# Experts' transposes inside the preceding products, and five weight splits behind the first fetch

## The chip, the cores and the metric

The kernel runs on one core of a Trainium2 chip. A core has TensorE (PE; its weight loads are shown as PEld), VectorE (DVE), ScalarE (ACT), GpSimd (POOL) and SyncE (SP, which here only issues DMAs). Each engine works through its own queue in order. The metric is the time of one execution in device microseconds, as the median of several runs.

## The reference

One layer of an encoder for 1024 tokens of width 1024: a mixer (attention to a memory, a convolution module and a bidirectional RWKV-7), then a mixture of 16 experts that choose their tokens, then a last norm. The change touches the experts:

```
def expert_choice_ffn(h, w_router, w_gate, w_up, w_down):
    cap = CAPACITY_FACTOR * S // N_EXPERTS                 # 128 tokens per expert
    aff = softmax(h @ w_router)
    gates, idx = top_k(swapaxes(aff, 1, 2), cap)
    xe = h[idx]                                            # per expert 128 x 1024
    hid = silu(xe @ w_gate) * (xe @ w_up)                  # 1024 x 1024 each
    ye = (hid @ w_down) * gates
    return zeros_like(h).at[idx].add(ye)
x = x + expert_choice_ffn(rms_norm(x))
return rms_norm(x, final_norm_g)
```

## The kernel before, in words

The first part (to about 840 us) computes the mixer and the router's products. Then VectorE picks each expert's tokens, and the 16 experts follow one another.

**One expert.** `fetch` (L1411) makes a one-hot matrix `oneh` on VectorE, multiplies it on PE with the tokens' numbers and gates (L1418), copies the numbers to `idx` and the gates to `gates` on VectorE (L1419, L1420), and lets GpSimd gather the expert's 128 rows into `xe` (L1422). `transposed` (L1428) turns 128 rows into columns: per half four PE transposes into a PSUM buffer of tag `A` (of which there are two), a ScalarE copy for the high part (L1436) and a VectorE subtraction for the low part (L1437). Rows become `xh`, `xl` (two buffers), activations `fh`, `fl` (one). There are three products per expert: gate, up and down. Each has eight k steps, and a k step has six matmuls of 512 columns, since every factor is held as a high and a low fp32r part (`mm3`, L330): high with high (L331), high rows with low weights (L332), low rows with high weights (L333).

**The weights.** `order_w` lists all weight blocks in the order of use: gate of expert 0, then for each expert e up(e), gate(e+1), down(e). SP fetches 1 MB blocks into 12 `eraw` buffers; a fetch waits until its buffer's former block has been split. `parts` (L1342) is a generator that splits the next 128 x 1024 weights: ScalarE makes `ewh` (L1355, L1351), VectorE makes `ewl` (L1356), and for down weights VectorE and GpSimd take turns (L1352). There are `NWB = 5` pairs of `ewh` and `ewl`, so splits run at most five k steps ahead of PE. The first five splits are drawn at L1360, ahead of the choice of tokens.

**The order of the loop** (L1536 on), for expert e: up product, `hid` times up on VectorE (L1545), transposes of the rows of e+1, `fetch(e+2)`, gate product of e+1 with its Silu (L1458), transposes of `hid` (inside `down`), down product of e, scaling (L1471) and the scatter that adds into `x2_d` (L1472). The last gate product is done in two pieces of four k steps; between them stand expert 14's down product and `last_loads`, which reads all rows back from `x2_d` behind expert 14's scatter, with the last weights behind that on SP's queue. Then come the last up and down products and the norm.

**What sets the order.** The kernel is traced in program order, and the compiler's scheduler gives each engine the first traced instruction that it estimates to be ready, so that the order within an engine can differ from that of the code. `tc.keep_in_program_order` and `tc.manual_schedule` take that freedom away. `product` (L1440) takes a dictionary `then`: what stands under k is traced behind step k.

Of the kernel before, what the change touches and what calls it, by code (L numbers as in the profile page):

```python
# [20 lines left out]
P = 128  # L21
# [78 lines left out]


@with_exitstack
def hybrid_block_kernel(ctx: ExitStack, tc: tile.TileContext, x, xT, memT, memn, w_in, w_mk, w_mv, pcols,
# [14 lines left out]
    # ---------------------------------------------------------------- constants  # L118
# [16 lines left out]
    # mask of the within-chunk matrices, [rows s (twice), {strict, inclusive}, t]  # L135
    mask = const.tile([P, 2, C], F32, name="mask")
    V.memset(mask, 1.0)
    for hf in range(2):
        r = slice(hf * 64, hf * 64 + 64)
        for q in range(2):  # L140
            # keeps t - s - 1 + q >= 0
            G.affine_select(out=mask[r, q, :], in_=mask[r, q, :], pattern=[[1, C]], compare_op=ALU.is_ge, fill=0.0,
                            base=q - 1, channel_multiplier=-1)
# [8 lines left out]
    # masks that put the inverses of the diagonal blocks in place: [row, parity, block column]  # L152
# [19 lines left out]
    # identity columns as the lanes of the inversion hold them: [lane (quadrant, parity, chunk), sigma, t]  # L172
# [5 lines left out]
    # derived per-channel columns  # L178
# [27 lines left out]
    def rsqrt(dst, src, scale, eps):  # L206
        """dst = (src * scale + eps) ** -0.5: a first guess from the exponent, then Newton's steps."""
# [18 lines left out]
    def run(mains, fills):  # L226
        """mains: names in order; fills: name -> (pieces, number, first, last, needs); pieces of fills are spread over
        the mains' steps. needs: (own piece, name, count)"""
# [24 lines left out]
    # tiles that live through the whole first part  # L253
# [4 lines left out]
    # ---------------------------------------------------------------- projections  # L258
# [16 lines left out]
    # the even taps, the odd ones, and their sums  # L275
# [59 lines left out]
    # memory: keys and values  # L335
# [3 lines left out]
    def memory():  # L339
# [15 lines left out]
        # a bank's first product alone starts it: where nothing was written yet, the others' first ones do not add  # L355
# [76 lines left out]
    def ev_shift(nm, j):  # L432
        st = {}

        def f(ps, n, sl):
# [6 lines left out]
            if n == 1:  # L442
# [3 lines left out]
                if nm in shifted:  # L446
                    # rows 64-127 belong to the backward scan: reversed time
# [8 lines left out]
                if nm == "gd":  # L456
                    # twice the sigmoid
# [15 lines left out]
    # the first two projections follow the loads  # L473
# [30 lines left out]
    # ---------------------------------------------------------------- convolution  # L504
# [3 lines left out]
    def taps(eng, i, j):  # L508
        """one of the three half-rate filters of a tile of channels: even taps on even tokens, odd on odd, and
        their sums on neighbours' sums"""  # L510
# [17 lines left out]
    def conv():  # L528
        for i in range(3):
# [8 lines left out]
            # even tokens, then odd ones  # L538
# [50 lines left out]
    def keep(i, n):  # L589
        """a part of the mixers' output, split in two, to DRAM"""  # L590
# [8 lines left out]
    # ---------------------------------------------------------------- attention  # L599
# [47 lines left out]
    # ---------------------------------------------------------------- RWKV-7  # L647
    # The backward scan is the forward one on reversed time: its tiles hold time reversed, so one step serves both.
# [7 lines left out]
    def early():  # L656
        """what the first chunks need, in the room of the convolution and the attention"""
# [9 lines left out]
        # zeros stand where one head's rows meet the other head's columns  # L667
# [10 lines left out]
        # restart marks of the running sums  # L678
# [6 lines left out]
    def late():  # L685
        """the rest, in the room of the projections"""
# [6 lines left out]
        # of these two, the last half pair needs the second only  # L693
# [9 lines left out]
    def swap():  # L703
        """room for the output projection, for the last half pair"""
# [29 lines left out]
    def chunks(ap, d):  # L734
        """[P, 512] as [P, chunk, t], in the time of direction d"""
# [5 lines left out]
    def spread(rs):  # L741
        """[P tokens, 4 tiles, head] to [channels, 512 tokens] in PSUM"""
# [8 lines left out]
    def columns(src, two, ps=None):  # L751
        """512 tokens' products with two columns, tokens on partitions"""
# [24 lines left out]
    def prep(p, k, g):  # L777
# [7 lines left out]
        for d in range(2):  # L785
# [23 lines left out]
            # 1/P overwrites the running sums  # L809
# [4 lines left out]
            # -kk a / P  # L814
# [807 lines left out]
```

## Time and profile before

| what | value |
|---|---|
| median of 3 runs | 1528.49 us (1524.61 to 1532.74) |
| profiled execution, first to last instruction | 1526.2 us |
| PE busy | 1341.4 us, 88% |
| VectorE busy | 1230.6 us, 81% |
| ScalarE busy | 841.9 us, 55% |
| GpSimd busy | 458.8 us, 30% |
| DMA | 327.92 MB, mean 215 GB/s |

The profile gives no other time for the profiled execution than its span; the span lies inside the range of the three runs. Busy shares are means over two unlike parts, so they say little of the experts, which begin at about 840 us and have their own rows below. Matmuls are pipelined: the time from one start to the next tells how fast PE goes, not the duration of one.

### The profile page before, as it was taken

How to read it: one execution, taken by the hardware profiler on the slowest of the kernel's cores; microseconds unless marked ns; L12 is line 12 of the kernel's file. 1: busy time of each engine (PE TensorE's matmuls, PEld its weight loads, DVE VectorE, ACT ScalarE, POOL GpSimd, SP SyncE). 2: the span in 40 equal slices, each digit the busy share in tenths (PEclk: the TensorE clock that was granted, in tenths of full speed). 3: DMA queues.
4: the chain of work that ended last, by engine and by line, in shares of the span. 5: the costliest groups of instructions: out<-in, count | busy, mean ns of one | idle time of the engine just before them, and what ended most of it. 6: DMA issues, size and time to landing. Idle time of an engine off the chain costs nothing.

```text
span 1526.2 us, 24448 instructions
## 1 busy us (share of the span) xinstructions
PE 1341.4 (88%) x9254; PEld 1074.2 (70%) x9254; DVE 1230.6 (81%) x2071; ACT 841.9 (55%) x1209; POOL 458.8 (30%) x302
## 2 busy tenths in 40 slices
PE   6988999996889898788999279999999999999984
PEld 4776658675777777667778167777777777777763
DVE  8899975698686979697534879888888888888887
ACT  4222574434435353424312358888888888888872
POOL 2233313432121213121211004444444444444323
PEclk9998899997897988899899679999999999999996
DMA  8222113313443524333525769999999999999855
GB/s 287 73 63 65 57 63 130 126 56 117 115 139 96 155 93 137 105 111 116 206 115 227 297 223 329 367 361 361 365 367 361 368 370 355 364 365 368 323 174 225
DMA packets 146101, 327.92 MB, mean 215 GB/s; under 512 B 9792, under 2 KB 64960, under 8 KB 145984
## 3 DMA queue, kind: packets, MB, share of 16 engines
q1 hardware_dynamic: 139360, 303.14, 55.3%
q0 software_dynamic: 6192, 22.55, 5.2%
q8 instruction: 72, 1.18, 0.3%
q10 hardware_dynamic: 432, 0.68, 0.1%
q14 instruction: 45, 0.37, 0.1%
HBM read 288.58 MB, written 37.75 MB: 214 GB/s over the span
## 4 chain that ended last, share of the span: by engine, by line
PE 55%; DVE 23%; ACT 8%; DMA 6%; issue 5%; POOL 1%; SPq 0%; POOLq 0%; DVEq 0%; ACTq 0%
PE mm L331 14%; PE mm L333 14%; PE mm L332 13%; DVE cv L519 3%; DVE dtmp L912 3%; DVE Dt L913 2%; DMA fo<-oT_d 2%; ACT Ld L897 2%; DVE ewl L1356 1%; ACT hid L1458 1%; ACT ewh L1351 1%; PE mm L1167 1%; PE mm L747 1%; DMA eraw<-in_w_ed_dram 1%; PE psA L856 1%
## 5 line engine op out<-in xcount | busy, mean ns | idle before, releaser
L1356 DVE SCALAR_TENSOR_TENSOR ewl<-eraw,pc,ewh 128x1024 fp32r<-128x1024 f32 x256 | 336.3, 1362 | 20.4 <-ACT ewh L1355 18.8
L1355 ACT ACTIVATE ewh<-eraw,pc 128x1024 fp32r<-128x1024 f32 x256 | 290.4, 1152 | 72.2 <-PE mm L333 70.1
L1352 POOL TENSOR_TENSOR ewl<-eraw,ewh 128x1024 fp32r<-128x1024 f32 x64 | 183.6, 2874 | 131.9 <-ACT ewh L1351 115.8
L331 PE MATMUL mm<-ewh,xh 128*128 128x512 f32 x512 | 201.6, 394 | 12.6 <-ACT xh L1436 12.6
L332 PE MATMUL mm<-ewl,xh 128*128 128x512 f32 x512 | 199.8, 390 | 0.0
L333 PE MATMUL mm<-ewh,xl 128*128 128x512 f32 x512 | 198.1, 392 | 0.1
L1351 ACT ACTIVATE ewh<-eraw 128x1024 fp32r<-128x1024 f32 x128 | 136.0, 1064 | 44.9 <-PE mm L333 39.0
L1352 DVE TENSOR_TENSOR ewl<-eraw,ewh 128x1024 fp32r<-128x1024 f32 x64 | 122.5, 1915 | 35.6 <-ACT ewh L1351 34.2
L331 PE MATMUL mm<-hh,wh 128*128 128x512 f32 x304 | 127.2, 419 | 9.8 <-ACT hh L312 9.8
L333 PE MATMUL mm<-hh,wl 128*128 128x512 f32 x304 | 126.5, 416 | 0.8 <-POOL wl L327 0.8
L332 PE MATMUL mm<-hl,wh 128*128 128x512 f32 x304 | 126.5, 416 | 0.4 <-DVE hl L313 0.3
L331 PEld LDWEIGHTS mm<-ewh,xh 128*128 128x128 f32 x512 | 96.3, 188 | 36.2 <-ACT xh L1436 16.5
L331 PE MATMUL mm<-ewh,fh 128*128 128x512 f32 x256 | 102.7, 403 | 14.3 <-ACT fh L1436 8.5
L332 PEld LDWEIGHTS mm<-ewl,xh 128*128 128x128 f32 x512 | 96.4, 188 | 19.6
L333 PEld LDWEIGHTS mm<-ewh,xl 128*128 128x128 f32 x512 | 95.0, 188 | 19.5 <-DVE xl L1437 0.6
L332 PE MATMUL mm<-ewl,fh 128*128 128x512 f32 x256 | 102.1, 399 | 7.0 <-DVE ewl L1352 7.0
L333 PE MATMUL mm<-ewh,fl 128*128 128x512 f32 x256 | 99.1, 397 | 1.8 <-DVE fl L1437 1.8
L327 POOL TENSOR_TENSOR wl<-wraw,wh 128x512 fp32r<-128x512 f32 x38 | 59.1, 1559 | 126.7 <-ACT wh L326 109.0
L1422 POOL DMA_INDIRECT xe<-h_d,idx x16 | 29.4, 1836 | 217.0 <-DVE gates L1420 217.0
L967 POOL TENSOR_TENSOR sps<-S,pcs 128x128 f32<-128x128 f32 x48 | 22.8, 474 | 218.7 <-DVE S L993 115.4
L331 PEld LDWEIGHTS mm<-hh,wh 128*128 128x128 f32 x304 | 60.1, 198 | 26.2 <-ACT hh L312 10.4
L332 PEld LDWEIGHTS mm<-hl,wh 128*128 128x128 f32 x304 | 60.0, 197 | 18.5 <-DVE hl L313 3.0
(412 smaller groups left out, 3011.2 us busy)
## 6 DMA issues: line engine op xcount, KB each, us to landing
eraw<-in_w_eg_dram SPq DMA_DIRECT2D x64, 1024.0 KB, 8.6
eraw<-in_w_eu_dram SPq DMA_DIRECT2D x64, 1024.0 KB, 9.2
eraw<-in_w_ed_dram SPq DMA_DIRECT2D x64, 1024.0 KB, 5.7
fo<-oT_d SPq DMA_DIRECT2D x64, 320.0 KB, 3.9
wraw<-in_w_in_dram SPq DMA_DIRECT2D x38, 256.0 KB, 2.7
ld_k<-d_k SPq DMA_DIRECT2D x18, 256.0 KB, 3.3
ld_v<-d_v SPq DMA_DIRECT2D x18, 256.0 KB, 3.1
xk<-in_xT_dram SPq DMA_DIRECT2D x16, 256.0 KB, 4.7
```

Source lines behind the costliest of these rows:

```text
L327: G.tensor_sub(wl, raw, wh.bitcast(F32))
L331: T.matmul(ps, lhsT=lh, rhs=rh, start=first, stop=False)
L332: T.matmul(ps, lhsT=lh, rhs=rl, start=False, stop=False)
L333: T.matmul(ps, lhsT=ll, rhs=rh, start=False, stop=last)
L519: V.scalar_tensor_tensor(o[:, 0:ln], z, w, o[:, 0:ln], op0=ALU.mult, op1=ALU.add)
L897: A.copy(Ld[r_, :, c:c + 4].rearrange("p t c -> p c t"), g["AM", d, q][r_, :, h, 0, b * 32:b * 32 + 32])
L912: IE.tensor_tensor(tmp[:, sg, ts], lcol, drow, op=ALU.mult)
L913: IE.tensor_tensor(Dt[:, sg, ts], Dt[:, sg, ts], tmp[:, sg, ts], op=ALU.add)
L1351: A.activation(h, raw[a], AF.Copy)
L1352: eng.tensor_sub(l, raw[a], h.bitcast(F32))
L1355: A.activation(h, raw[a], AF.Copy, scale=gain)
L1356: V.scalar_tensor_tensor(l, raw[a], gain, h.bitcast(F32), op0=ALU.mult, op1=ALU.subtract)
```

## The change

The transposes of expert e+1's rows are traced behind step 3 of expert e's up product, those of expert e's activations behind step 2 of the gate product of e+1, and `fetch(e+2)` behind its step 0. The first five weight splits are drawn in `fetch(0)`, and `tc.issue_after` puts those of their instructions that run on VectorE behind the reduction that writes `gates` for expert 0. The rest of the diff takes out comments.

```diff
+KTX, KTF, KTH = 3, 0, 2
...
     parts = parts()
-    split = [next(parts) for _ in range(NWB)]
+    split = []
...
-        V.tensor_reduce(gates[:, :, e], ps[:, 1:5].rearrange("p (a b) -> p a b", b=2), axis=AX.X, op=ALU.add)
+        gs = V.tensor_reduce(gates[:, :, e], ps[:, 1:5].rearrange("p (a b) -> p a b", b=2), axis=AX.X, op=ALU.add)
...
         if e == 0:
             tc.keep_in_program_order(g)
+
+            with tc.issue_after(gs.ins):
+                split.extend(next(parts) for _ in range(NWB))
         return xe
...
-    def gate(e, xs, between=None):
+    def gate(e, xs, then=None, between=None):
         ga = [mm("cx") for _ in range(2)]
         if between:
-            product(ga, *xs, ks=range(2 * BRK))
+            product(ga, *xs, then, ks=range(2 * BRK))
             between()
-        product(ga, *xs, ks=range(2 * BRK if between else 0, KT))
+        product(ga, *xs, then, ks=range(2 * BRK if between else 0, KT))
...
-    def down(e, done, then=None):
-        hs = transposed(done, "f")
+    def down(e, hs, then=None):
...
-    def add_back(e, done):
-        dn = down(e, done)
+    def add_back(e, hs):
+        dn = down(e, hs)
...
-    rows = [fetch(0), fetch(1)]
-    cur = transposed(rows.pop(0), "x")
-    hid = gate(0, cur)
+    rows = {0: fetch(0), 1: fetch(1)}
+    xs, hs = {0: transposed(rows[0], "x")}, {}
+
+    def turn_x(e):
+        xs[e] = transposed(rows.pop(e), "x")
+
+    def turn_h(e, done):
+        hs[e] = transposed(done, "f")
+
+    def bring(e):
+        rows[e] = fetch(e)
+
+    hid = gate(0, xs[0])
     for e in range(NE):
         up = [mm("y0"), mm("y1")]
-        then = None
+
         if e == NE - 1:
...
-        product(up, *cur, then)
+        else:
+            then = {KTX: [lambda: turn_x(e + 1)]}
+        product(up, *xs.pop(e), then)
...
         if e + 1 < NE:
-            cur = transposed(rows.pop(0), "x")
+            then = {KTF: [lambda: bring(e + 2)] if e + 2 < NE else [], KTH: [lambda: turn_h(e, done)]}
             if e + 2 < NE:
-                rows.append(fetch(e + 2))
-                hid = gate(e + 1, cur)
-                add_back(e, done)
+                hid = gate(e + 1, xs[e + 1], then)
+                add_back(e, hs.pop(e))
             else:
-                hid = gate(e + 1, cur, lambda: (add_back(e, done), last_loads()))
+                hid = gate(e + 1, xs[e + 1], then, lambda: (add_back(e, hs.pop(e)), last_loads()))
         else:
...
-            dn = down(e, done, then)
+            dn = down(e, transposed(done, "f"), then)
```

## Rows read from the trace of the kernel before

**Rows 1.** The view by stretches: two experts. Start:end, length, busy (count), granted clock, DMA.
```profile
1118.60:1156.20 37.60, 36.17 (x170) 29.58 (x169) 33.27 (x30) 30.78 (x34) 15.58 (x7) 1.00 1.01 365
1381.90:1419.50 37.60, 36.16 (x170) 29.56 (x169) 32.39 (x29) 30.76 (x33) 15.45 (x7) 1.00 0.99 368
```
**Rows 2.** The lists of waits, 968 to 1419 us: all engines, then SP's queue.
```profile
DVE ewl L1352 <- ACT ewh L1351: 27.2, 29, 1.5
DVE ewl L1356 <- ACT ewh L1355: 12.3, 24, 0.7
DVE idx L1419 <- PE mm L1418: 6.6, 12, 0.5
DVE fl L1437 <- ACT fh L1436: 5.2, 12, 0.5
...
SPq L1250 <- DVE ewl L1356: 245.3, 96, 4.4
```
**Rows 3.** PE's timeline from one up product into the next gate product.
```profile
1131.34 0.39 PE L331 MATMUL mm<-ewh,xh 128*128 128x512 f32 x1
...
1142.22 1.03 PE L1434 MATMUL mm<-ident,xe 128*128 128x128 f32 x8
1144.11 0.50 PE L331 MATMUL mm<-ewh,xh 128*128 128x512 f32 x1 [0.85 <-ACT xh L1436]
...
1145.34 1.05 PE L1418 MATMUL mm<-tokaff,oneh 128*128 128x6 f32 x8
1146.25 0.71 PE L333 MATMUL mm<-ewh,xl 128*128 128x512 f32 x2
1146.80 0.39 PE L331 MATMUL mm<-ewh,xh 128*128 128x512 f32 x1
```
**Rows 4.** PE's timeline from the gate product into a down product.
```profile
1118.74 1.03 PE L1434 MATMUL mm<-ident,hid 128*128 128x128 f32 x8
1120.33 0.50 PE L331 MATMUL mm<-ewh,fh 128*128 128x512 f32 x1 [0.55 <-ACT fh L1436]
...
1121.82 0.39 PE L331 MATMUL mm<-ewh,fh 128*128 128x512 f32 x1
```
**Rows 5.** PE's timeline around the last gate product's first piece.
```profile
1450.88 1.03 PE L1434 MATMUL mm<-ident,hid 128*128 128x128 f32 x8
...
1455.62 0.72 PE L333 MATMUL mm<-ewh,fl 128*128 128x512 f32 x2 [1.75 <-DVE fl L1437]
1456.18 0.40 PE L331 MATMUL mm<-ewh,fh 128*128 128x512 f32 x1
```
**Rows 6.** The opening: PE's timeline, VectorE's timeline, and the chain that ended last.
```profile
880.09 1.84 PE L1418 MATMUL mm<-tokaff,oneh 128*128 128x6 f32 x8 [2.25 <-DVE oneh L1414]
...
879.86 6.06 DVE L1356 SCALAR_TENSOR_TENSOR ewl<-eraw,pc,ewh 128x1024 fp32r<-128x1024 f32 x5
885.84 0.15 DVE L1419 CAST idx<-mm 128x1 int32<-128x1 f32 x1
...
889.22 0.16 DVE L1419 CAST idx<-mm 128x1 int32<-128x1 f32 x1 [2.03 <-PE mm L1418]
...
886.28 5.22 DMA xe<-h_d,idx
```
**Rows 7.** The end: the chain that ended last, and SP's timeline.
```profile
1467.17 6.86 DMA x_d<-ye,idx
...
1474.04 2.09 SPq L1493 DMA_DIRECT2D eraw<-x_d  x4
```
**Rows 8.** The view by stretches while the last loads queue.
```profile
1484.00:1488.00 4.00, 0.97 (x7) 0.50 (x5) 3.28 (x6) 2.98 (x5) 0.00 (x0) 0.67 1.02 408
```
**Rows 9.** One expert's down weights: SP's and ScalarE's timeline, and the list of DMA issues.
```profile
1043.61 10.45 SPq L1250 DMA_DIRECT2D eraw<-in_w_ed_dram  x4
...
1075.88 1.06 ACT L1351 ACTIVATE ewh<-eraw 128x1024 fp32r<-128x1024 f32 x1 [0.21 <-PE mm L333]
...
eraw<-in_w_ed_dram SPq DMA_DIRECT2D x64, 1024.0 KB, 5.7
```

## The prediction

> **What bounds the kernel now.** I read the stages first, then the longest stage by engine, then what PE waits for in it. The page's 40 slices show two halves: up to some 840 us no engine is full, from there PE is at 9 tenths in nearly every slice. Those last 680 us are the experts, and the change lies there alone, so the rest is taken as unmoved. The view by stretches shows the experts alike: the one from 1118.6 us takes 37.60 us and the one from 1381.9 the same, with PE busy some 36.2 us and VectorE some 33 us [rows 1]. The reader is to see two engines and the DMA all near full, so it must be settled who sets the 37.6 us. The list of waits settles it: SP waited 245.3 us for buffers that VectorE frees after their split (of the 451 us from 968 to 1419), so weights are called for no faster than they are used up, and VectorE stood 27.2 + 12.3 us for ScalarE's copies, 6.6 us for PE's fetch products and 5.2 us for fh [rows 2]. Those copies wait in turn for PE to give a weight buffer back: VectorE's slack is PE's pace. PE is the bound, and what stops it is small and regular.
>
> Inside a product PE starts a 512-column matmul every 0.2267 us (48 in an up product, from 1131.34 to 1142.22). It does so until the next product needs transposed rows: then eight transposes, a stop for ScalarE's copy of 0.85 us, four matmuls, a second short stop for VectorE's xl, the fetch's eight products, and only from 1146.80 the regular step again [rows 3]. Before a down product it is the same with hid and a stop of 0.55 us [rows 4].
>
> **The change part by part.** (1) The rows' transposes. From 1142.22 to 1146.80 PE spends 4.58 us. In it are six regular matmuls (6 x 0.2267 = 1.36 us) and eight fetch products (1146.25 - 1145.34 = 0.91 us), which stay [rows 3]. The eight transposes stay too: they show 1.03 us busy, the last one's drain included; in a running product I take 0.95 us, from 0.85 (without that drain) to 1.03. What goes is 4.58 - 1.36 - 0.91 - 0.95 = 1.36 us. They now stand after k = 3 of the preceding up product, and four more k steps (4 x 6 x 0.2267 = 5.4 us) lie between transposes and use, against the 1.89 us that transposes and first copy took in the open. If that cover were gone, the 1.36 us would be back.
>
> (2) The activations' transposes. From 1118.74 to 1121.82 are 3.08 us, with six matmuls and eight transposes: 3.08 - 1.36 - 0.95 = 0.77 us go [rows 4]. They now stand after k = 2 of the gate product, 3 x 6 x 0.2267 = 4.1 us after the up product's end; VectorE's two hid products take 1.4 us there, so PE should not wait for them, and five k steps (6.8 us) cover the two copies and the two fl.
>
> Both happen 14 times with the fetch (experts 0 to 13): 14 x (1.36 + 0.77) = 29.8 us. The last expert's rows come without a fetch, and I take the same 1.4 us for them. Expert 14's activations, between the two pieces of the last gate product, take 5.30 us (1450.88 to 1456.18), since L333 waited 1.75 us for fl: 5.30 - 1.36 - 0.95 = 3.0 us [rows 5]. There only one k step is left as cover (1.36 us), so this term runs from 1 to 3 us.
>
> (3) The fetch of expert e+2 moves behind k = 0 of the gate product. PE already ran it behind four of that k's matmuls, though it is traced ahead of them: the compiler's scheduler moves work to where it judges it ready. I cost it at nothing. Its gather on POOL's queue leaves some 0.5 us later and is wanted a whole expert later; SP's queue is not passed. What stands behind its wait is VectorE's queue: idx waits for PE there as before, 0.55 us each (6.6 us over 12) [rows 2].
>
> (4) The opening. VectorE ran the five first splits from 879.86 to 885.9, and idx came at 885.84 although PE's fetch products had ended at 880.09 + 1.84 = 881.93; the gather landed at 886.28 + 5.22 = 891.5, and PE, ScalarE and VectorE all stood for it [rows 6]. Behind gates, idx can run at some 882.0: 3.87 us earlier, and with it the gather on POOL. The splits then end at about 882.3 + 6.1 = 888.4, while the first is wanted by PE at some 890: covered. SP's calls for the first w_ed blocks come some 2.5 us later and those are used 40 us on: nothing. Expert 1's oneh (VectorE) and fetch products (PE) now come behind the splits and may be put ahead of expert 0's transposes or its xl. Bounds: 0.2 us, if PE takes expert 1's eight products first (they ended at 889.2 behind a oneh, and would end near 891.4), and 3.87 us. I take 3.3, near the upper end, since the gather lands near 887.7, before that oneh is done, less half a oneh for xl's queueing.
>
> (5) The end. The last loads wait for expert 14's scatter: it is issued at 1467.17 and lands 6.86 us on, SP's loads of the rows leave at 1474.04, the last w_ed behind them [rows 7]. That chain hangs on expert 14's down product, which all savings above precede, so they pass through whole. What is late next is the same chain.
>
> Sum: 29.8 + 1.4 + 3.0 + 3.3 = 37.5 us. From it I take 0.2 us for each of 14 experts, 2.8 us, for weight parts that come late now and then: VectorE's 33.3 us in 35.5 instead of in 37.6 leave half the slack. 34.7 us remain. The profiled execution spans 1526.2 us, so 1491.5; the median of three runs stands 2.3 us above that span, and with the same distance the time is 1494 us.
>
> **DMA, row and page.** An expert moves 365 GB/s x 37.6 us = 13.7 MB; in 35.4 us that is 388 GB/s. The trace shows this rate and more: 408 GB/s while the last loads queue [rows 8]. The weights are also far ahead: w_ed blocks asked for from 1043.61 are first copied at 1075.88, 32 us later, with 5.7 us to land in the median and 8 to 10 where they queue [rows 9], so some 22 to 24 us of weights lie ready.
>
> The Trainium skill speaks against it: DMA: Bandwidth & Descriptors, section Specifications, gives some 358 GB/s from HBM for each core. By that figure an expert's 13.7 MB would need 38.3 us and the change could gain nearly nothing there. The trace disagrees: 365 GB/s in an expert and 408 in the queue [rows 1, 8], nearer to the 425 GB/s that the page's section Bandwidth lists for a core that streams alone.
>
> **The rivals.** *VectorE becomes the bound.* For: 33.3 of 37.6 us busy, and it stands in order at idx, xl and fl. Against: of its 4.3 us of waits the largest, for copies that PE paces, shrink as PE is faster. If half the 2.27 us (27.2 / 12) and all the 0.55, 0.43 and 1.0 stay, an expert takes 33.3 + 3.1 = 36.4 us: 14 x 1.2 = 16.8, and with the other 1.4 + 3.0 + 3.3 some 24.5 us gain: 1504 us.
>
> *DMA binds.* If 365 GB/s were the most it gives, each expert would fall 2.1 us behind, 29 us in 14; 24 us lie ready, 5 us are lost: 1499 us. Against it the 408 GB/s and SP's waits for buffers.
>
> *The order stays.* The scheduler places by its own estimates, as the fetch products show; transposes could land at the product's end again. Then only the opening gains: 1525 us, within 0.5%.
>
> *Slower.* VectorE's queue is in order, and idx, xl and fl each wait there for PE work that now stands in the middle of a product. The splits for the coming k steps stand behind them. In the opening such a wait held VectorE 2.03 us at idx [rows 6]. If all three held it 2.03 us in each expert, VectorE needs 33.3 + 6.1 = 39.4 us, 1.8 more than now: 14 x 1.8 = 25 us lost, 8 us gained by the other terms: 1545 us. It decides once these waits exceed some 4.9 us per expert (4.3 of idle time now, and 8 / 14). Against: five pairs of weight parts stand between VectorE and PE, and rows 3 show the waits at half a microsecond.
>
> **How the numbers follow.** Forecast 0.62, VectorE 0.13, DMA 0.05, order stays 0.10, slower 0.10. A difference under 0.5% (7.6 us) can't be told from none, with three runs from 1524.6 to 1532.7. Faster by more: 0.80; within: 0.10; slower: 0.10. The range: all upper bounds (0.1 us for each of 30 transposes, 0.6 in the opening, the 2.8 us not lost) give 41 us, 1487, and a microsecond of scatter 1486; the top takes in VectorE and DMA with 6 us above: 1510.
>
> **What would show it.** Right: an expert period near 35.5 us; transposes between matmuls with no idle row after them; idx at 882; the last scatter 35 us earlier. Wrong: L332 waiting for ewl inside products, VectorE's idle rows at xl or fl above a microsecond, weight DMAs whose landing time grows from expert to expert, or a granted clock under 1.00 in the experts.

## The result and the profile after

The changed kernel takes 1550.31 us in the median of five runs (1546.66 to 1560.72); the kernel before, on the same chip, 1528.49 us (1524.01 to 1533.53). The ratio is 1.0145, 95% interval 1.0108 to 1.0181: slower by some 22 us, where 34 us of gain were forecast. L numbers of after are 2 above those of before in the helpers (PE L333 to L335, splits L1354 and L1358), later ones some 4 to 16.

The profiled execution is the longest of the five (1560.72 us, span 1558.9), so stages are compared, not spans. Up to expert 0's fetch VectorE, ScalarE, GpSimd and SP have the same order of instructions as before, and PE the same instructions, and there the profiles scatter for themselves: idx of expert 0 comes between 874.7 and 891.5 us in the fifteen profiles that have the new opening. From expert 0's fetch products on, the traces divide so:

| stage (start of fetch 0's products, first weight matmul, first scatter, fifteenth scatter, end) | before | after | difference |
|---|---|---|---|
| fetch products to first weight matmul | 13.4 | 12.9 | -0.5 |
| to the first scatter | 50.8 | 57.0 | +6.2 |
| first to fifteenth scatter (14 periods) | 522.9 | 537.8 | +14.9 |
| to the end | 59.0 | 61.6 | +2.6 |

The sum, +23.2 us, is near the 21.8 us between the medians. A period is the time from one scatter to the next. Before, all but the first and last take 37.6 us. After, they are 38.3 to 38.4 us up to the eighth scatter, then 37.7, 40.3, 39.8, 39.6, 39.7, 38.5 and 33.6 us.

The view by stretches of after, an early period and a late one (columns as in [rows 1]: VectorE is the third busy time, GpSimd the fifth; the number behind it is the mean granted clock of PE):

```profile
1036.30:1074.70 38.40, 36.31 (x170) 29.40 (x169) 37.70 (x30) 30.64 (x33) 16.39 (x7) 1.00 0.98 357
...
1304.70:1344.30 39.60, 37.27 (x171) 29.22 (x170) 34.56 (x33) 29.20 (x33) 17.42 (x7) 1.00 0.98 358
```

In the early one VectorE is busy 37.70 of 38.40 us, 4.4 us more than in [rows 1] for the same work, at a full granted clock of PE. In the late one no engine is full, at a full clock too: there engines wait for each other.

PE's timeline of that early expert, the answer to [rows 3] (rows' transposes, at 1078.66) and [rows 4] (activations', at 1051.65):

```profile
1051.65 1.03 PE L1439 MATMUL mm<-ident,hid 128*128 128x128 f32 x8
1052.44 0.48 PE L333 MATMUL mm<-ewh,xh 128*128 128x512 f32 x1
...
1059.34 0.39 PE L333 MATMUL mm<-ewh,fh 128*128 128x512 f32 x1
...
1062.06 0.39 PE L333 MATMUL mm<-ewh,fh 128*128 128x512 f32 x1
1063.89 0.50 PE L334 MATMUL mm<-ewl,fh 128*128 128x512 f32 x1 [1.44 <-DVE ewl L1354]
...
1067.23 0.50 PE L334 MATMUL mm<-ewl,fh 128*128 128x512 f32 x1 [0.33 <-DVE ewl L1354]
...
1070.57 0.50 PE L334 MATMUL mm<-ewl,fh 128*128 128x512 f32 x1 [0.32 <-DVE ewl L1354]
...
1073.21 0.39 PE L333 MATMUL mm<-ewh,xh 128*128 128x512 f32 x1
...
1078.66 1.03 PE L1439 MATMUL mm<-ident,xe 128*128 128x128 f32 x8
1079.45 0.48 PE L333 MATMUL mm<-ewh,xh 128*128 128x512 f32 x1
```

The moved transposes do what was forecast: eight of them, 0.79 us from start to start, and no idle entry behind either set. What is new lies in the down product: 1059.34 to 1073.21 are 13.87 us for 48 matmuls that need 48 x 0.2267 = 10.88. The 2.99 us too many are the whole of 38.4 - 35.4, and the entries name the low halves of the down weights.

VectorE's and GpSimd's timelines of the same stretch, the line that makes those halves being L1354 on both:

```profile
1055.91 1.22 DVE L1354 TENSOR_TENSOR ewl<-eraw,ewh 128x1024 fp32r<-128x1024 f32 x1
1057.05 3.44 DVE L1416 TENSOR_TENSOR oneh<-slots,posT 128x1024 fp32r<-128x1024 f32 x1
1060.41 10.10 DVE L1354 TENSOR_TENSOR ewl<-eraw,ewh 128x1024 fp32r<-128x1024 f32 x3
```
```profile
1056.66 9.44 POOL L1354 TENSOR_TENSOR ewl<-eraw,ewh 128x1024 fp32r<-128x1024 f32 x3 [5.25 <-DMA eraw<-in_w_eg_dram]
1066.49 2.95 POOL L1354 TENSOR_TENSOR ewl<-eraw,ewh 128x1024 fp32r<-128x1024 f32 x1 [0.39 <-ACT ewh L1353]
```

The subtraction that VectorE starts 0.75 us ahead of GpSimd's first takes 1.22 us. From there on, while both run, each of VectorE's takes 3.4 us, oneh too, and GpSimd's 3.1 us; GpSimd's shortest in the trace of before (such as the one at 1123.16, with VectorE idle in its first half) took 2.40 us. Two parts, one from each engine, then come out every 3.4 us, and PE uses two in 2 x 6 x 0.2267 = 2.72 us. The view of these lines for 1000 to 1200 us (least, median and greatest duration in ns), before and after:

```profile
L1352 DVE TENSOR_TENSOR ewl<-eraw,ewh x24: 1216/1814/2600, 1002.5 to 1199.7; 128x1024 fp32r<-128x1024 f32 x24
L1352 POOL TENSOR_TENSOR ewl<-eraw,ewh x23: 2403/2726/3387, 1003.3 to 1198.4; 128x1024 fp32r<-128x1024 f32 x23
```
```profile
L1354 DVE TENSOR_TENSOR ewl<-eraw,ewh x20: 1217/3416/3425, 1017.6 to 1182.2; 128x1024 fp32r<-128x1024 f32 x20
L1354 POOL TENSOR_TENSOR ewl<-eraw,ewh x20: 2727/3149/3381, 1018.3 to 1181.6; 128x1024 fp32r<-128x1024 f32 x20
```

The first pair was there to be read before the prediction: one shape, on one engine, with a median 1.5 times its least. The Trainium skill, SBUF — State Buffer, section Who interferes with whom, says that a VectorE instruction with two inputs in SBUF contends with a GpSimd instruction that reads SBUF. The trace agrees: VectorE's takes 1.22 us where it is alone, 3.4 us beside GpSimd's.

The list of waits, answering to [rows 2] (977 to 1428 us, all engines, then SP's queue):

```profile
ACT ye L1475 <- PE mm L335: 21.8, 5, 5.9
...
PE mm L334 <- DVE ewl L1354: 14.5, 21, 1.4
...
ACT fh L1441 <- PE mm L1439: 13.2, 5, 3.0
DVE ewl L1358 <- ACT ewh L1357: 11.8, 7, 5.5
...
PE mm L334 <- POOL ewl L1354: 7.0, 14, 1.1
DVE idx L1421 <- PE mm L1420: 5.8, 5, 1.7
...
DVE fl L1442 <- ACT fh L1441: 4.0, 7, 0.6
...
SPq L1252 <- DVE ewl L1358: 214.7, 83, 5.1
```

PE now stops inside products for parts from both engines, which it did not do in that stretch before. The rows with 5 counts, ye and fh, come from the late experts: ScalarE stood up to 5.9 us at ye and 3.0 us at fh, with weight parts queued behind. SP still waits for buffers most of the time, so weights are not short.

The opening, answering to [rows 6] (VectorE's, then PE's timeline):

```profile
891.50 0.16 DVE L1421 CAST idx<-mm 128x1 int32<-128x1 f32 x1 [2.02 <-PE mm L1420]
...
891.64 6.06 DVE L1358 SCALAR_TENSOR_TENSOR ewl<-eraw,pc,ewh 128x1024 fp32r<-128x1024 f32 x5
897.62 1.22 DVE L1416 TENSOR_TENSOR oneh<-slots,posT 128x1024 fp32r<-128x1024 f32 x1
```
```profile
889.63 1.83 PE L1420 MATMUL mm<-tokaff,oneh 128*128 128x6 f32 x8 [2.25 <-DVE oneh L1416]
898.99 1.84 PE L1420 MATMUL mm<-tokaff,oneh 128*128 128x6 f32 x8 [7.52 <-DVE oneh L1416]
900.68 1.97 PE L1439 MATMUL mm<-ident,xe 128*128 128x128 f32 x8
```

idx comes 1.87 us behind the start of the products instead of 5.75, as forecast, but PE takes expert 1's products ahead of expert 0's transposes, and those wait for a oneh behind the five splits. That is the case of the lower bound.

The end, answering to [rows 5] (expert 14's transposes) and [rows 7]: PE's, then SP's timeline.

```profile
1476.85 1.03 PE L1439 MATMUL mm<-ident,hid 128*128 128x128 f32 x8
1477.64 0.48 PE L334 MATMUL mm<-ewl,xh 128*128 128x512 f32 x1
...
1519.79 1.22 PE L333 MATMUL mm<-ewh,xh 128*128 128x512 f32 x2 [5.36 <-ACT ewh L1357]
```
```profile
1503.26 2.09 SPq L1497 DMA_DIRECT2D eraw<-x_d  x4
1505.46 0.42 SPq L1252 DMA_DIRECT2D eraw<-in_w_eu_dram  x1
```

Expert 14's activations are turned without a stop, too. But the last block of the up weights is now called for behind the rows, and PE waits 5.36 us for it.

### The profile page after: what moved, and what is told of

Read it like the earlier page. It is cut to its first block, busy times and chain, and to the rows that moved or that the text cites. A ratio compares the mean times of both kernels' runs of the same rounds, so it can differ in the third digit from the quotient of the medians.

```text
span 1558.9 us, 24454 instructions
## 1 busy us (share of the span) xinstructions
PE 1364.0 (87%) x9254; PEld 1082.8 (69%) x9254; DVE 1261.0 (81%) x2071; ACT 832.3 (53%) x1209; POOL 473.8 (30%) x302
## 4 chain that ended last, share of the span: by engine, by line
PE 41%; DVE 26%; DMA 11%; issue 11%; ACT 6%; POOL 6%; SPq 0%; POOLq 0%; DVEq 0%; ACTq 0%
PE mm L334 9%; PE mm L335 9%; PE mm L333 8%; DVE ewl L1354 4%; POOL ewl L1354 3%; DVE cv L521 3%; DVE ewl L1358 3%; DMA eraw<-in_w_eg_dram 2%; DVE dtmp L914 2%; DVE Dt L915 2%; DMA eraw<-in_w_ed_dram 2%; ACT Ld L899 2%; DMA fo<-oT_d 2%; PE psA L858 1%; DMA eraw<-in_w_eu_dram 1%
## 5 line engine op out<-in xcount | busy, mean ns | idle before, releaser
L1358 DVE SCALAR_TENSOR_TENSOR ewl<-eraw,pc,ewh 128x1024 fp32r<-128x1024 f32 x256 | 322.4, 1312 | 34.6 <-ACT ewh L1357 33.3
L1357 ACT ACTIVATE ewh<-eraw,pc 128x1024 fp32r<-128x1024 f32 x256 | 283.9, 1148 | 50.7 <-PE mm L335 45.9
L1354 POOL TENSOR_TENSOR ewl<-eraw,ewh 128x1024 fp32r<-128x1024 f32 x64 | 197.5, 3101 | 195.6 <-issue 99.6
L335 PE MATMUL mm<-ewh,xl 128*128 128x512 f32 x512 | 201.1, 393 | 0.0
L333 PE MATMUL mm<-ewh,xh 128*128 128x512 f32 x512 | 192.1, 400 | 9.2 <-ACT ewh L1357 9.2
L1354 DVE TENSOR_TENSOR ewl<-eraw,ewh 128x1024 fp32r<-128x1024 f32 x64 | 151.2, 2387 | 12.9 <-ACT ewh L1353 12.9
L1353 ACT ACTIVATE ewh<-eraw 128x1024 fp32r<-128x1024 f32 x128 | 130.4, 1056 | 30.3 <-PE mm L335 28.1
L333 PE MATMUL mm<-hh,wh 128*128 128x512 f32 x304 | 128.0, 421 | 9.6 <-ACT hh L314 9.6
L334 PE MATMUL mm<-ewl,fh 128*128 128x512 f32 x256 | 107.7, 421 | 32.2 <-DVE ewl L1354 21.1
L335 PE MATMUL mm<-hh,wl 128*128 128x512 f32 x304 | 127.4, 419 | 4.7 <-POOL wl L329 4.7
L333 PEld LDWEIGHTS mm<-ewh,xh 128*128 128x128 f32 x512 | 96.6, 190 | 31.3 <-ACT ewh L1357 12.1
L335 PEld LDWEIGHTS mm<-ewh,xl 128*128 128x128 f32 x512 | 97.1, 190 | 19.9 <-DVE xl L1442 0.2
L329 POOL TENSOR_TENSOR wl<-wraw,wh 128x512 fp32r<-128x512 f32 x38 | 65.5, 1726 | 131.8 <-ACT wh L328 114.2
L335 PE MATMUL mm<-ewh,fl 128*128 128x512 f32 x256 | 101.1, 396 | 0.7 <-DVE fl L1442 0.7
L333 PE MATMUL mm<-ewh,fh 128*128 128x512 f32 x256 | 98.2, 397 | 0.0
L334 PEld LDWEIGHTS mm<-ewl,fh 128*128 128x128 f32 x256 | 48.9, 191 | 62.2 <-DVE ewl L1354 33.5
L333 PEld LDWEIGHTS mm<-hh,wh 128*128 128x128 f32 x304 | 60.8, 200 | 25.8 <-ACT hh L314 9.6
```

Source lines behind the costliest of these rows:

```text
L329: G.tensor_sub(wl, raw, wh.bitcast(F32))
L333: T.matmul(ps, lhsT=lh, rhs=rh, start=first, stop=False)
L334: T.matmul(ps, lhsT=lh, rhs=rl, start=False, stop=False)
L335: T.matmul(ps, lhsT=ll, rhs=rh, start=False, stop=last)
L1353: A.activation(h, raw[a], AF.Copy)
L1354: eng.tensor_sub(l, raw[a], h.bitcast(F32))
```

## The experiments

All kernels are the changed one with the edit shown, except b_nopool (the kernel before). Ratios are to the kernel before, timed beside each.

**No down split on GpSimd.** GD is the number of splits of which one goes to GpSimd.

```diff
-GD = 2
+GD = 1000
```

> The changed kernel with all splits of the down weights on VectorE, none on GpSimd. Theory (port): in the changed kernel VectorE's splits with two SBUF inputs and GpSimd's take turns, 3.4 us for each pair where PE needs 2.7 us for its two k steps; without GpSimd's an expert falls from 38.4 us to about 36 us and the whole to 1510 to 1525 us. Rival (VectorE is short of time): it gets 4 x 1.2 us more for each expert, the period stays at 38 us or grows, 1550 us or more. Rival (order): where the later experts' order costs most, their 39.7 us stay and the whole falls to no less than 1535 us.

> The kernel before with all splits of the down weights on VectorE. Port theory: PE's own stops set the 37.6 us, VectorE's splits get shorter without GpSimd beside them, so nothing much changes: 1522 to 1532 us. Rival (VectorE is short of time): 4 x 1.2 us more in each expert, half of it in the idle time that was there, some 1545 us.

a_nopool: 1501.64 us, ratio 0.9789 (0.9772 to 0.9805), below the 1510 to 1525 us forecast. b_nopool: 1522.37 us, ratio 0.9924 (0.9907 to 0.9941), with periods of 37.6 us as before. So it is not GpSimd's share in itself but its meeting with the new order: the same edit takes 3.6% of the time before from the changed kernel (1.0145 to 0.9789) and 0.8% from the old one. The stretch of one early expert of a_nopool, and its down splits on VectorE:

```profile
1012.00:1047.40 35.40, 35.40 (x170) 29.58 (x169) 33.68 (x33) 30.64 (x33) 3.47 (x3) 1.00 1.02 383
```
```profile
L1354 DVE TENSOR_TENSOR ewl<-eraw,ewh x45: 1218/1221/1224, 999.5 to 1182.1; 128x1024 fp32r<-128x1024 f32 x45
```

PE is busy 35.40 of 35.40 us, and VectorE with all eight splits (33.68) less than with four in the changed kernel (37.70). But behind expert 8 the periods rise to 39.5, 37.4 and 36 us: a second cause.

**oneh out of the way, and the rows' transposes put back.** In a_oneh, the next oneh is traced behind the fetch products:

```diff
+        if 1 <= e < NE - 1:
+            hot[e + 1] = one_hot(e + 1)
```

In a_nox, the rows are transposed between the products again:

```diff
-            then = {KTX: [lambda: turn_x(e + 1)]}
+            then = None
...
+            turn_x(e + 1)
```

> The changed kernel, with the next expert's oneh traced right behind the fetch products, so that VectorE makes it before GpSimd's splits begin. Port theory: oneh took 3.4 us in the midst of GpSimd's splits and 1.2 us alone, so the first eight experts win about 2 us each (36.3 us a period), the later ones little: 1532 to 1538 us. Rival (the splits alone fill the time): no change, 1548 to 1552 us.

> The changed kernel with the rows' transposes back between the products, the activations' still inside. Its order of work stays the regular one up to expert 13. Port theory: oneh falls before GpSimd's splits and VectorE catches up while PE stands for the rows, so some 36.8 to 37.2 us a period and 1518 to 1526 us. Rival (the activations' place is what costs): 38 us a period or more, 1540 us or more.

a_oneh: 1556.11 us, ratio 1.0141 (1.0109 to 1.0173), periods of 38.4 us: oneh's 3.4 us were not the cause; four splits of VectorE then fill the same 13.5 us beside four of GpSimd's. (The piece to the first scatter shortens from 57.0 to 53.0 us, and late periods reach 47.4.) a_nox: 1564.11 us, ratio 1.0173 (1.0131 to 1.0216): a miss, and the rival's period of 38 us or more came true. Three periods of it in the view by stretches:

```profile
1150.13:1188.37 38.24, 36.25 (x170) 29.44 (x169) 35.97 (x30) 30.96 (x33) 17.20 (x6) 1.00 0.99 358
1188.37:1228.20 39.83, 37.84 (x170) 30.50 (x169) 35.97 (x30) 30.95 (x33) 17.14 (x6) 0.96 0.96 343
1228.20:1269.60 41.40, 39.45 (x170) 32.05 (x169) 36.03 (x30) 30.99 (x33) 17.00 (x7) 0.92 0.93 331
```

At a full granted clock a period is 38.2 us, no longer than in the changed kernel: GpSimd's four splits still take 12.7 us beside VectorE's, and PE's stops of 0.85 us at xh and 0.93 us at xl are back. The other 1.6 and 3.2 us are the clock, which stood at the lower of its two levels (1.2 instead of 2.4 GHz) for a part of those periods, right behind PE's stops at xh and xl. So a_nox's time says less of the transposes than its period at full clock does.

**The activations' transposes put back.** a_noh leaves out the other half:

```diff
-            then = {KTF: [lambda: bring(e + 2)] if e + 2 < NE else [], KTH: [lambda: turn_h(e, done)]}
+            then = {KTF: [lambda: bring(e + 2)] if e + 2 < NE else []}
...
-    def down(e, hs, then=None):
+    def down(e, done, then=None):
+        hs = transposed(done, "f")
```

> The changed kernel with the activations' transposes alone put back to the head of the down product (rows' transposes still inside the up product), GpSimd with its four down splits. PE's stop of 0.77 us per expert is back: 14 x 0.77 = 11 us of PE's own time. Theory (VectorE's and GpSimd's down splits hold each other up when they run side by side): fl again stands between VectorE's down splits, so that fewer of them meet one of GpSimd's; the mean of VectorE's down split falls from 3.4 us toward the 1.8 us of before and the period of experts 1 to 7 to some 37 us, 1530 us. Rival (the loss comes from transposes in the middle of products, which would be half undone): period 38.4 + 0.77 = 39.2 us if the rows' transposes cause it, 36.3 us if the activations' do, with VectorE's splits as long as in the changed kernel.

1531.24 us, ratio 0.9999 (0.9963 to 1.0035). Periods of 36.2 us for experts 1 to 8, which is 37.6 less the 1.4 us forecast for the rows; then 37.6 to 41.6, all at a full clock. The theory had 37 us; the rival's 36.3 us is nearer, but it wanted VectorE's splits as long as in the changed kernel, and their median fell from 3.42 to 2.35 us (1000 to 1200 us). VectorE's timeline in one of its down products:

```profile
1108.62 1.21 DVE L1354 TENSOR_TENSOR ewl<-eraw,ewh 128x1024 fp32r<-128x1024 f32 x1
1109.76 1.21 DVE L1416 TENSOR_TENSOR oneh<-slots,posT 128x1024 fp32r<-128x1024 f32 x1
1111.16 3.16 DVE L1354 TENSOR_TENSOR ewl<-eraw,ewh 128x1024 fp32r<-128x1024 f32 x1 [0.19 <-ACT ewh L1353]
1114.24 1.28 DVE L1442 TENSOR_TENSOR fl<-mm,fh 128x512 fp32r<-128x512 f32 x2
1115.60 2.08 DVE L1354 TENSOR_TENSOR ewl<-eraw,ewh 128x1024 fp32r<-128x1024 f32 x1
1118.39 2.64 DVE L1354 TENSOR_TENSOR ewl<-eraw,ewh 128x1024 fp32r<-128x1024 f32 x1 [0.71 <-ACT ewh L1353]
```

The splits meet GpSimd's here too (3.16, 2.08, 2.64 us), but fl stands between them, and from the first split to the last it is 12.4 us instead of 14.6; PE, which stops 0.55 us for fh before it starts on them, waits for none. I read this as the use of PE's stop: it gave the splits time. No run shows that reading by itself. That the splits can meet and cost PE nothing is the limit of the theory as I had it.

**One input instead of two.** In a_one VectorE's four down splits read one tile.

```diff
-                    eng.tensor_sub(l, raw[a], h.bitcast(F32))
+                    if eng is G:
+                        G.tensor_sub(l, raw[a], h.bitcast(F32))
+                    else:
+                        V.tensor_scalar(l, h.bitcast(F32), 1.0 / 8192, None, op0=ALU.mult)
```

> The changed kernel, with VectorE's four down splits replaced by a multiplication that reads one tile instead of two (the low halves of those weights are then a scaled copy of the high halves, so part of the computation is changed); GpSimd's four subtractions of two tiles stay. Theory (VectorE and GpSimd hold each other up where VectorE reads two tiles of SBUF): VectorE's instruction falls from 3.42 us to 1.3 us or less beside GpSimd's, GpSimd's from 3.1 to some 2.5 us, and the period of experts 1 to 7 from 38.4 to 35.4 or 36 us. Rival (any VectorE work on such tiles meets GpSimd's, by the room or the engine's write): 3.4 us and 38.4 us as before.

1532.24 us in one run; periods of 35.4 us for experts 1 to 7, as forecast, but not for the reason given. VectorE's line there:

```profile
L1357 DVE TENSOR_SCALAR ewl<-ewh x24: 685/2316/2783, 1004.4 to 1188.8; 128x1024 fp32r<-128x1024 f32 x24
L1355 POOL TENSOR_TENSOR ewl<-eraw,ewh x24: 2849/2857/3342, 1005.1 to 1191.0; 128x1024 fp32r<-128x1024 f32 x24
```

It takes 0.69 us alone and 2.3 us beside GpSimd: it waits as well, only each pair is done in about 2.9 us instead of 3.4. My clause on two inputs is wrong for this instruction. The Trainium skill, SBUF — State Buffer, section Who interferes with whom, lists tensor_scalar among the operations that can take the pair of ports which VectorE shares with GpSimd, and so can contend with it. The trace agrees with that, by the 2.3 us.

**The order written out.** The scheduler's order of the queues changes behind expert 8 in the changed kernel: ScalarE gets ye ahead of parts that it made before ye until then. a_pin holds PE's moved work behind its k step and ScalarE's Silu and ye behind four parts (shown for Silu); a_np_pin does it with GD = 1000.

```diff
+    def behind_parts(n=4):
+        split.extend(next(parts) for _ in range(n - len(split)))
+        return tc.issue_after(made[0].ins)
...
-                for f in then[k]:
-                    f()
+                with tc.issue_after(end.ins):
+                    for f in then[k]:
+                        f()
...
+        with behind_parts():
+            for n in range(2):
+                A.activation(hid[:, n * 512:(n + 1) * 512], ga[n], AF.Silu, scale=gates[:, 1, e:e + 1])
```

> The changed kernel with its order written out: every transposition and fetch stands on PE right behind the k step that it was traced behind, and ScalarE makes four weight parts before each Silu and before each ye, in all experts alike; GpSimd keeps its four down splits. If the shared splits set the period of experts 1 to 7 (38.4 us) and a drifting order that of the later ones (37.7 to 40.3 us, mean 39.3 us over experts 8 to 13), the period is 38.4 us throughout, the six later ones give back 6 x 0.9 = 5 us, and the time is 1545 us. If the order alone were the cause of the loss, the period falls to 35.5 us and the time to 1500 us. If the order does nothing, it stays at 1550 us with later periods of up to 40 us.

> The same written order, and all down splits on VectorE (GpSimd has none). Without the order this kernel took 1501.6 us, with periods of 35.4 us for experts 1 to 8 and 35.9 to 39.5 us behind them. Theory (shared splits first, order second): 35.4 us throughout; the later experts give back 4.1 + 2.0 + 0.5 + 0.5 + 0.9 = 8 us, so 1494 us. Rival (the later periods are VectorE's load or the weights that come late, not the order): 39 us periods return after some 300 us of experts, 1501 us.

a_pin: 1560.98 us, ratio 1.0193 (1.0167 to 1.0219), late periods up to 40.9 us; a_np_pin: 1505.24 us, 0.9847 (0.9826 to 0.9868), late ones 36.8 to 38.4. Both miss. But from the same expert on, the copies xh and fh had moved ahead of parts in ScalarE's queue, so the order was not yet regular: in a_np_pin ScalarE stood 2.85 us at xh and 4.96 us at fh in an expert.

**Two ends.** a_best is a_np_pin with expert 1's fetch behind expert 0's transposes, and NLR = 6, by which SP calls for the last up block ahead of the rows.

```diff
+    with tc.issue_after(turned_[0].ins):
+        rows[1] = fetch(1)
...
-NLR = 5
+NLR = 6
```

> As the run before (order written out, no down split on GpSimd), and two ends mended: expert 1's fetch is held behind the transposes of expert 0's rows, and the fourth block of the last up weights is asked for ahead of the loads of all rows. Theory: the opening gives 3.3 us (its transposes no longer wait for expert 1's fetch products, which stand behind five splits and a oneh), the end up to 2.5 us (PE's wait of 5.36 us for that block shrinks): 1494 - 5.8 = 1488 us. Rival: both are covered by other work, PE then waits for weight parts in the opening and for the rows at the end: 1494 us as without them.

1509.53 us, ratio 0.9839 (0.9774 to 0.9903): no gain that can be told. In the trace the first weight matmul starts 9.53 us behind the start of the fetch products instead of 12.91, the 3.4 us forecast; but the piece to the first scatter grows from 48.7 to 50.8 us, so 1.3 us are left. Some 0.9 us of that growth are expert 1's eight fetch products, which now stand in this piece; its mean clock also fell from 0.98 to 0.96. The tail stays (60.0 by 59.2 us): PE no longer waits for that block of the up product (5.4 us in a_np_pin), but 4.7 and 3.8 us for parts in the down product, so SP's order alone does not shorten the end.

**Both queues in order.** a_ord (GpSimd's four splits) and a_best2 (a_best with it) also issue the copies xh and fh behind the fifth part ahead; a_best4 is a_best2 with GD = 4.

```diff
-            A.activation(h[:, s_, :], ps, AF.Copy)
+            with behind_parts(5 if inside else 0):
+                A.activation(h[:, s_, :], ps, AF.Copy)
```

> As a_pin, and ScalarE's two copies of transposed rows and the two of transposed activations are issued behind the fifth weight part ahead of PE as well, so that its queue has in all experts the order that it had in the first eight of a_pin (where that changed, from expert 8 on, its queue stood 2.85 us for rows and 4.96 us for activations in an expert, in the trace of a_np_pin, with weight parts waiting behind it). Theory (queue order sets the later periods, the shared down splits those of 38.4 us): the periods of 39.2 to 40.9 us become 38.4 us, a gain of 0.8 + 4 x 2.5 + 1.4 = 12 us: 1549 us by a_pin's 1561 us. Rival (something else grows with time, such as weights that come late or the clock): the periods behind expert 8 stay near 40.9 us, 1561 us.

> As a_best, with the same order of ScalarE's queue. a_best has 35.4 us for experts 1 to 8 and 38.5, 37.0, 38.4, 37.1 and 36.8 us behind them. Theory (queue order): 35.4 us up to expert 13, a gain of 3.1 + 1.6 + 3.0 + 1.7 + 1.4 = 10.8 us, so 500.6 - 10.8 = 490 us from the first to the last scatter and a ratio to the kernel before of 0.984 - 0.007 = 0.977. Rival (VectorE, at 33.7 of 35.4 us without GpSimd's help, falls behind in the long run): periods grow again behind some expert and the ratio stays at 0.984.

> As a_best2, but two of the eight down splits of each expert on GpSimd instead of none (the changed kernel has four). Theory (a down split of VectorE that meets one of GpSimd's takes 3.4 us instead of 1.22 us, so that GpSimd takes little off VectorE): each of the two lengthens one or two of VectorE's by 2.2 us and saves 1.22 us, and PE waits in the down product, as it has 2.7 us for two parts: 35.4 + 1 to 2 us each expert, 14 to 28 us slower than a_best2. Rival (only the alternation of four and four is at fault, or VectorE is short of time): as fast as a_best2 or faster, 35.4 us.

a_ord: 1555.38 us, ratio 1.0169 (1.0119 to 1.0218), late periods up to 44.1. a_best2: 1504.67 us, 0.9834 (0.9786 to 0.9883), late ones 36.6 and 38.2. a_best4: 1519.02 us, 0.9944 (0.9879 to 1.001), 35.4 us early against my forecast (two splits on GpSimd are hidden), 38 to 43 late. All miss in the late experts. The list of waits of a_best2 from 1230 to 1390 us shows what came in there; none of these rows stands in its list of 1000 to 1160 us:

```profile
DVE hid L1573 <- PE mm L335: 10.1, 5, 2.0
DVE idx L1425 <- PE mm L1424: 5.9, 5, 1.2
...
PE mm L334 <- DVE ewl L1358: 4.7, 5, 0.9
```

With ScalarE's queue held, VectorE's had changed, at the same expert: hid now stood ahead of parts that it used to follow. The waits are not all of it, as two of the late periods show:

```profile
1264.06:1300.62 36.56, 35.63 (x170) 29.50 (x169) 32.55 (x33) 30.60 (x33) 3.43 (x2) 1.00 0.96 356
1300.62:1338.82 38.20, 37.27 (x170) 30.61 (x169) 34.69 (x34) 30.58 (x33) 4.24 (x2) 0.96 1.00 372
```

A late period at a full clock is 1.2 us longer than an early one (36.56 by 35.37), and 0.93 us of that is a stop of PE for a part of L1358. The other 1.6 us, where they occur, are the granted clock, which fell right behind such a stop. Late periods of a_oneh, a_one, a_pin, a_np_pin, a_best, a_ord and a_best4 show clocks of 0.92 to 0.97 as well. In the changed kernel's 14 periods it is 1.00, so there the clock has no part. Not every stop is followed by a fall: a_noh's longest period, 41.6 us, is at 1.00.

The last three kernels hold VectorE's order too:

```diff
+            with behind_parts(4 if e + 1 < NE else 0, 1):
+                V.scalar_tensor_tensor(hid[:, sl], up[n], gates[:, 1, e:e + 1], hid[:, sl], op0=ALU.mult, op1=ALU.mult)
```

> As a_best2, and VectorE's two products of the up product (hid) are issued behind its third weight part ahead of PE, in all experts. In a_best2 they stand without any part ahead of them from expert 9 on: VectorE waited there 2.0 us for PE at hid in each expert (10.1 us over five, none before), 1.2 us at idx, with the parts behind, and the period rose from 35.4 to 36.6 to 38.2 us just there. Theory (the order of the in-order queues, now regular on both engines): 35.4 us up to expert 13, the last some 31 us, so 13 x 35.4 + 31 = 491 us from the first to the last scatter instead of 507.7, and a ratio to the kernel before of 0.983 - 0.011 = 0.972. Rival (something that grows with time, such as weights that come later from expert to expert): the periods rise behind expert 8 as in a_nopool, a_np_pin, a_best and a_best2, 504 us or more, ratio 0.983.

> As a_noh (rows' transposes inside the up product, activations' at the head of the down product, GpSimd with four down splits), with the order of ScalarE's and VectorE's queues made regular in the same way. a_noh had 36.2 us for experts 1 to 8, which is the period of before less the 1.4 us of the rows' transposes, and 37.6 to 41.6 us behind them, where its queues change their order. Theory: 36.2 us up to expert 13, 13 x 36.2 + 34 = 505 us from the first to the last scatter instead of 521.5 (before: 522.9), and some 1514 us. Rival as above: 521 us, 1531 us.

> The whole change with GpSimd's four down splits, with the regular order of both queues. a_ord had periods that alternate between 36.3 and 38.5 us up to expert 8 (mean 37.4 us, as the splits of VectorE and GpSimd meet or miss each other) and 39.2 to 44.1 us behind. Theory (the shared splits set the first, the order the second): 36.3 to 38.5 us up to expert 13, 13 x 37.4 + 34 = 520 us from the first to the last scatter instead of 551.5, 1524 us. Rival (order is no cause, GpSimd's splits get slower with time): as a_ord, 551 us and 1555 us.

| kernel | GpSimd's splits | median us | ratio (interval) | first to fifteenth scatter | forecast of it | periods but the last |
|---|---|---|---|---|---|---|
| a_best5 | 0 of 8 | 1484.82 | 0.9722 (0.9691 to 0.9753) | 490.6 | 491 | 35.4 throughout |
| a_noh5 | 4 of 8 | 1507.60 | 0.9881 (0.9829 to 0.9933) | 501.7 | 505 | 36.2 to 36.4 |
| a_ord5 | 4 of 8 | 1527.14 | 0.9989 (0.9963 to 1.0016) | 521.1 | 520 | 36.3 to 38.6, then 38.2 to 35.4 |

a_best5's stretches, early and late:

```profile
1082.00:1117.40 35.40, 35.40 (x169) 29.60 (x169) 33.94 (x34) 30.63 (x33) 3.43 (x2) 1.00 1.02 389
1365.20:1400.60 35.40, 35.40 (x170) 29.50 (x169) 32.86 (x33) 30.58 (x33) 3.44 (x2) 1.00 1.02 384
```

With both queues held nothing grows with time: the late periods came from the order of two in-order queues, with the stops of PE and the falls of the clock that followed. a_best5 beats the kernel before and every other kernel here.

## Why the prediction was wrong

**What failed** is the one term by which the forecast paid for VectorE: "0.2 us for each of 14 experts, 2.8 us, for weight parts that come late now and then: VectorE's 33.3 us in 35.5 instead of in 37.6 leave half the slack". It took VectorE's busy time as fixed. It is not: moved work changed which splits run beside GpSimd's, and the busy time rose to 37.70 us. That term measured 30.5 us over 14 periods (a_ord5's 521.1 less a_best5's 490.6, which differ in GpSimd's splits and, at the ends, in the two edits of a_best). In expert 0, where the piece to the first scatter grew by 6.2 us, PE waits 4.8 us for VectorE's low halves of the down weights, which it did not before; 3.6 us of that are one stop, and from 949.0 to 955.7 us the granted clock stood at half, so that the piece's mean is 0.92 (before 0.99). That is some 4 us more, an estimate from 0.08 x 57.0 less 0.01 x 50.8.

**What was left out**: the scheduler's order of the other queues. I weighed that it might keep the transposes out of the products, but not that a fixed place on PE shifts what ScalarE and VectorE do, and only from expert 8 on. It costs 16.7 us (537.8 in the changed kernel, 521.1 in a_ord5): some 10 in the late experts, and the rest early, where a_ord5's periods go by turns. In those of 36.6 us GpSimd's four splits take 13.4 us, in those of 38.5 us 15.4 us, and there PE waits 1.9 us for them; VectorE's run beside them in both, so "meet or miss each other", as I had expected of it, is not what tells them apart. The three add up to the loss: 30.5 + 16.7 - 32.3 = 14.9 us over the 14 periods, the 32.3 us being what the moved transposes gave where nothing ate it.

**Steps (1) and (2) were right in size.** 37.6 - 36.2 = 1.4 us per expert for the rows (a_noh; 1.36 forecast), 37.6 - 35.4 = 2.2 us for both (a_best5; 2.13). First to fifteenth scatter fell by 522.9 - 490.6 = 32.3 us (a_best5). The last of these periods holds the rows of the last expert and expert 14's activations, forecast at 1.4 + 3.0 us; it fell from 33.55 to 30.39, 3.2 us, so 1.2 us of the two terms did not come; the 3.0 was the upper end of its own 1 to 3 us. **Step (3)**, the fetch at nothing, shows nothing against it in a_best5. **Step (4)**: it came out near the lower bound (0.5 us measured, 0.2 the bound, 3.3 taken), by the order that the prediction names for it; held apart, the 3.4 us appear at the first matmul. At the first scatter 1.3 us of it stay in a_best, 2.7 in a_best5 (61.6 us from the start of the fetch products in a_np_pin, 58.9 in a_best5). **Step (5)**: the end was to pass all savings on; the tail was 59.0 us before, 61.6 after and 54.7 in a_best5. What shortens it there is not separated: a_best2 has 54.6 us already, a_best 60.0, and between them only the copies' order differs; b_nopool has 54.1.

**The rivals.** "Slower", at 1545 us, came nearest in time, by another mechanism: waits at idx, xl and fl were to cost 6.1 us per expert and measured (5.8 + 4.0 + 1.6) / 12, about 1 us. "VectorE becomes the bound" named the engine and missed the cause: the bound was VectorE and GpSimd slowing each other. DMA did not bind: in a_best5, at up to 389 GB/s, SP stood 219.3 + 120.4 of the 400 us from 1000 to 1400 for buffers that VectorE's splits free. The Trainium skill (DMA: Bandwidth & Descriptors, section Specifications) gives some 358 GB/s from HBM for each core; the trace disagrees, as the prediction had said. "The order stays" did not occur: the transposes stood where they were traced.

## What to carry to other kernels

Before busy times are added up for a faster schedule, compare the least and the median duration of one shape on VectorE: a gap says that something beside it slows it at times (here GpSimd), and that the busy time can change with the order. A regular stall of the bounding engine can be what lets a neighbour catch up; price what it hides before it is removed. In a scheduled kernel, an edit's effect on the order of every queue has to be read over all iterations, since a pattern can hold for eight and then tip. And compare periods at the same granted clock: part of what a stop costs can come behind it, as a stretch at the lower level.

## What the runs showed of the hardware

VectorE's 128x1024 subtraction took 1.22 us alone (a_nopool) and 3.42 us beside GpSimd's, which took 3.1 us there and 2.40 us at the least in the kernel before; the two engines together then finish two parts in 3.4 us, and VectorE alone does two in 2.4 us. So GpSimd's help made the pair slower than VectorE by itself. A one-input multiplication went from 0.69 to 2.3 us the same way (a_one). DMA kept up 383 to 389 GB/s through whole experts (a_nopool, a_best5). In the experts the granted clock of PE fell from 2.4 to 1.2 GHz for a stretch behind a stop of 0.93 us in a_best2, and such a stretch made a period 1.6 us longer (38.20 by 36.56 us); behind other stops, as in a_noh, it stayed.
